# The last pass and the end of a fp32 decoder layer: last units bank by bank, layer norm by blocks of tokens, rows of x1 put in order in DRAM, and the mLSTM state products spread over the main products

## The chip, the cores and the metric

One NeuronCore of a Trainium2 chip. The metric is the device time of one execution in microseconds (us). The kernel is written instruction by instruction: a scheduler in Python fixes, at build time, the order of instructions on each engine (TensorE = PE, VectorE = DVE, ScalarE = ACT, GpSimd = POOL, and SyncE = SP, which only issues DMAs here). On the chip each engine runs its list in order and waits on semaphores.

## The reference

One layer on 320 tokens (256 of a prompt, 64 = 8 sequences × 8 of a sample batch), D = 2048, all float32. Cut to what matters:

```python
proj = x @ w_in                      # split: mLSTM q,k,v,i,f,o; HGRN2 q,f,i,g; two gates
h, C, n, m = _mlstm(q, k, v, ig, lf, C0, n0, m0)     # 4 heads, dk 256, dv 512, chunks of 64
o, S = _hgrn2(hq, log f, 1 - f, i, S0)               # 8 heads, dk 128, dv 256
merged = sigmoid(gate_a) * (branch_a @ w_branch_a) + sigmoid(gate_b) * (branch_b @ w_branch_b)
x1 = layernorm(alpha * x + merged @ w_out)
hid = square(relu(x1 @ w_up))                        # 2048 -> 8192
y = layernorm(alpha * x1 + hid @ w_down)             # 8192 -> 2048
# outputs: y, and the new states C, n, m, S of prompt and sample
```

For the prompt the new states are `C = k_scaled^T v` and `S = k_scaled^T i` over all 256 tokens: one product over the tokens for each head.

## The kernel before, in words

**Products.** A float32 product is done as three products of rounded halves: each operand is split into a high and a low part, and high×high, high×low and low×high are summed in a PSUM bank. The weights come from DRAM in tiles of 128 × 1024 (512 KB) into six raw buffers, all by SP's queue (`reload`). ACT writes the high half (`highs`, by the helper at L415), DVE the low half (`lows`, L681). The (high, low) pairs lie in a small pool, `wh`, `wl` and `bb` in the names below. `give` says where a pair's buffer goes once PE is done with it: back to the pool, or, near the end, to the pools for k and v (`kx`, `vx`).

**Main products.** `run_main` walks a list of units: first weight tiles of the projections ("w"), then the MLP with down projections in passes p = 0 to 7. The first seven passes have the kinds A, B and C (a scheme with seven products instead of eight, summed up later by `combine`). The last pass has the kinds D and E: 16 units in the order D g0 ×4, E g0 ×4, D g1 ×4, E g1 ×4, where g is a half of the output columns. Each such unit has one weight tile and 16 products of 512 columns into three PSUM banks: 4 for the samples' tokens (block 2), 6 for tokens 0 to 127 (block 0) and 6 for tokens 128 to 255 (block 1). Four units share three banks, so each bank is complete only in the fourth unit. `ev_last` then adds a bank to the sum of the earlier passes, adds the residual's part (put there by `residual`) and takes the statistics; `norm` (L2457 to L2467) applies the layer norm and stores y, once for the samples' block and once for both prompt blocks together, after the last statistics.

**x1 for the residual.** x1 is kept in DRAM (`xD`), written from a transposed layout, so that a token's row lies there in pieces of 32 floats (128 bytes). `residual` fetches the rows back with twelve DMAs of such pieces on SP's queue at the start of the last pass, and g2 and b2 with two more.

**States.** k and v of the four mLSTM heads and the operands of the eight HGRN2 heads also wait in DRAM (`kD`, `vD`, `sD`, `iD`). `m_C(h)` asks for k (L1370) and v (L1373) by POOL's queue when `kx` and `vx` have buffers, then waits until the main products are done (`main_end`), and does 12 products of 512 columns; `C_out` copies a bank by ACT and stores it by SP. `h_S(h)` does S of a head in four products of 256 columns, and it waits for C of all four heads.

**Order.** Each of these functions is a chain, a Python generator that yields an engine, a cost and an instruction, or a wait. The scheduler places ready chains by priority beside the main products, and the estimated times it works with fix the order only. They put no waiting time into the program. POOL's queue carries nothing but a few memsets and the loads of k and v.

Of the kernel before, what the change touches and what calls it, by code (L numbers as in the profile page):

```python
# [8 lines left out]
F32 = mybir.dt.float32  # L9
# [327 lines left out]
PE_C = 2000.0  # L337
PE_H = 1250.0


# [36 lines left out]
class Program:  # L377
# [312 lines left out]
    def run_main(self):  # L690
# [3 lines left out]
        for u, unit in enumerate(UNITS):  # L694
            if unit[0] != "w":
                self.down(u, *unit)
                continue
# [40 lines left out]
    def down(self, u, kind, p, g, i):  # L738
        s = self.s
        if (kind, g, i) == ("A", 0, 0) and p == 0:  # L740
            s.spawn(self.open_dn(), 0)
        if (kind, p, g, i) == ("A", PH - 2, 0, 0):
            for j in range(2):
                s.spawn(self.combine(j), 1)
        if (kind, g, i) == ("D", 0, 0):
            self.carve_end()
            now = s.t["pe"]
            self.vx.free.append((now, self.brest))
            self.kx.free += [(now, self.wxv[4].rearrange("p x s v -> p (x s v)")[:, 1024 * i:1024 * i + 1024]) for i in range(2)]
# [39 lines left out]
        s.pump(s.t["pe"])  # L789

    def take(self):
        s = self.s
        s.until(lambda: self.mbank.free)
        self.mbank.free.sort(key=lambda x: x[0])
        at, b = self.mbank.free.pop(0)
        s.t["pe"] = max(s.t["pe"], at)
        return b

    def give(self, u):

        now, hl = self.s.t["pe"], self.unit[u][0]
        n = [hl is w for w in self.wx].index(True) if any(hl is w for w in self.wx) else 0
        if n > 1 and u >= U_MLP - 6:
            if self.wide_done is None:
                self.wide_parts(self.wxv[n], now)
            else:
                self.wide_done.append(self.wxv[n])
        elif u >= len(UNITS) - 3 or n < 2 and any(hl is w for w in self.wx) and u > len(UNITS) - 16:
            if any(hl is w for w in self.wx):
                self.vx.free.append((now, self.wxv[n]))  # L810
            else:
                self.kx.free += [(now, x) for x in hl]
        elif self.hlp is not None:
            self.hlp.free.append((now, hl))
        else:
            self.hl_free.append((now, hl))
# [62 lines left out]
    def start(self):  # L879
# [22 lines left out]
        self.s_ev = {(x, c): Ev() for x in range(3) for c in range(4)}  # L902
        self.xD = self.dr.tile([32, 4, KT * TOK], F32, name="xD")
        self.used_ev = [Ev() for _ in range(KT)]
        first = d["first"]
# [461 lines left out]
    def m_C(self, h):  # L1367
        k = yield acq(self.kx)
        k = k.rearrange("p (x s k) -> p x s k", x=2, s=2)
        kt = yield ("pool", 1000, lambda: self.nc.gpsimd.dma_start(  # L1370
            k.rearrange("p x s k -> p (x s k)").rearrange("p (y k) -> p y k", k=128), self.kD[h].rearrange("y p k -> p y k")))
        w = yield acq(self.vx)
        vt = yield ("pool", 1000, lambda: self.nc.gpsimd.dma_start(w, self.vD[h]))  # L1373
        e = Ev()
        e.t = max(kt, vt) + 4000.0
        yield wait(e, self.main_end)
        for c in range(2):
            b = yield acq(self.mbank)
            for s in range(2):
                yield ("pe", 3 * pe_r(512), lambda: [self.mm(  # L1380
                    b, k.rearrange("p x s k -> p (x s k)")[:, 512 * x + 256 * c + 128 * s:512 * x + 256 * c + 128 * s + 128], w[:, y, s, :],
                    start=s == 0 and n == 0, stop=s == 1 and n == 2) for n, (x, y) in enumerate(((0, 0), (0, 1), (1, 0)))])
# [529 lines left out]
    def h_S(self, h):  # L1912
# [4 lines left out]
        e.t = t  # L1917
        yield wait(e, *[m["C"] for m in self.mh])
        b = yield acq(self.mbank)
# [324 lines left out]
    def spill_x1(self):  # L2244
# [11 lines left out]
        yield post(self.f3_ev)  # L2256

    def ev_up(self, T, p, b):
        v = self.nc.vector
# [118 lines left out]
    def residual(self):  # L2378

        v, d = self.nc.vector, self.d  # L2380
        T1, T2, TS = self.er
        x = self.xD.rearrange("r a (j b c) -> r (a j) b c", b=10, c=32)
# [20 lines left out]
        now = self.s.t["dve"]  # L2403
        self.sx.free += [(now, self.erest[:, 768 * i:768 * i + 768]) for i in range(6)]
        self.oS.free += [(now, self.erest[:, 4608 + 256 * i:4864 + 256 * i]) for i in range(2)]

# [22 lines left out]
    def ev_last(self, n, g, x, bank):  # L2429
# [7 lines left out]
        yield wait(self.w_ev[c][x])  # L2437
        rows = 128
        if x == 2:
            t = yield acq(self.ts)  # L2440
            rows = 64
            yield ("act", act(512), lambda: self.A(t[0:64], W[64:128]))
            yield ("dve", SUM, lambda: v.tensor_tensor(W[0:64], W[0:64], t[0:64], ALU.add))
            yield rel(self.ts, t)
        yield ("dve", SUM, lambda: v.bn_stats(self.st[:rows, x, c, :], W[:rows]))
# [4 lines left out]
    def norm(self, xs):  # L2450

        v = self.nc.vector
        yield wait(*[self.s_ev[x, c] for x in xs for c in range(4)])
        rows = 64 if xs == (2,) else 128
        n = len(xs)
        for x in xs:
            yield ("dve", 90, lambda: v.bn_aggr(self.mv[:rows, x, :], self.st[:rows, x].rearrange("p c n -> p (c n)")))  # L2457
        sm = yield acq(self.sm)
        yield from self.rsqrt(sm[:rows], self.mv[:rows, xs[0]:xs[0] + n, 1], n=n)
        G, B = self.gb2  # L2460
        for j, x in enumerate(xs):
            m, r = self.mv[:rows, x, 0:1], sm[:rows, 9 + n + j:10 + n + j]
            for c in range(4):
                W = self.last(c, x)[:rows]
                cc = slice(512 * c, 512 * c + 512)
                yield ("dve", SUM, lambda: v.scalar_tensor_tensor(W, W, m, G[:rows, cc], ALU.subtract, ALU.mult))
                yield ("dve", SUM, lambda: v.scalar_tensor_tensor(W, W, r, B[:rows, cc], ALU.mult, ALU.add))  # L2467
                yield ("sp", 620, lambda: self.dma(self.d["y"][128 * x:128 * x + rows, cc], W))

# [104 lines left out]
```

## Time and profile before

| | us |
|---|---|
| median of 3 runs | 2263.31 (2261.55 to 2263.45) |
| profiled execution: time | 2264.3 |
| profiled execution: span of instructions | 2262.5 |
| TensorE busy | 2247.8 (99%) |
| VectorE busy | 1687.1 (75%) |
| ScalarE busy | 1277.1 (56%) |
| GpSimd busy | 12.6 (1%) |
| mean granted TensorE clock | 0.997 |

The span runs from the first to the last instruction; the execution's time has 1.8 us more. TensorE's row is the one to watch: it is nearly always busy, so the kernel's time changes where TensorE waits or is slowed. The DMA engines moved 490.95 MB at a mean of 217 GB/s, nearly all by SP's queue (the row "q1"), 6.29 MB by POOL's (the row "q0").

### The profile page before, as it was taken

The numbers are of one execution on the slowest core, as the hardware profiler recorded it, in microseconds if no ns is written. First come the engines' busy times: TensorE is split into PE (matmuls) and PEld (weight loads), VectorE is DVE, ScalarE is ACT, GpSimd is POOL, SyncE is SP. The second block draws the span as 40 slices with busy tenths as digits, with TensorE's granted clock in tenths as the row PEclk, the third lists the DMA queues.
The fourth block names the chain that finished last, engine by engine and source line by source line (L and its number), as shares of the span: only waits on it lengthen the run. The fifth ranks groups of instructions, "written<-read, shape, count | busy, mean of one in ns | idle before, by whom it ended". The sixth has DMA issues, their size and how long they took to land.

```text
span 2262.5 us, 37822 instructions
## 1 busy us (share of the span) xinstructions
PE 2247.8 (99%) x14316; PEld 2135.7 (94%) x14316; DVE 1687.1 (75%) x2982; ACT 1277.1 (56%) x2339; POOL 12.6 (1%) x36
## 2 busy tenths in 40 slices
PE   9999999999999999999999999999999999999997
PEld 9999999999999999999999999999999999999986
DVE  5676777777777787655655769888888888888876
ACT  6666556678777766444434438564555455555442
POOL 0000000000000000000000000000000000000000
PEclk9999999999999999999999999999999999999998
DMA  7598888756666676555555645867667676666697
GB/s 285 168 266 256 270 275 247 240 179 189 192 190 201 189 218 179 173 173 173 173 172 189 199 142 167 279 235 229 235 223 239 225 243 223 238 227 242 218 268 248
DMA packets 265535, 490.95 MB, mean 217 GB/s; under 512 B 119300, under 2 KB 145540, under 8 KB 264072
## 3 DMA queue, kind: packets, MB, share of 16 engines
q1 hardware_dynamic: 260472, 482.05, 67.2%
q0 software_dynamic: 4736, 6.29, 1.1%
q8 instruction: 112, 1.84, 0.3%
q14 instruction: 71, 0.58, 0.1%
q10 hardware_dynamic: 144, 0.20, 0.0%
HBM read 434.93 MB, written 53.53 MB: 216 GB/s over the span
## 4 chain that ended last, share of the span: by engine, by line
PE 97%; ACT 1%; issue 1%; DMA 0%; DVE 0%; POOL 0%; POOLq 0%; ACTq 0%
PE bank L421 97%; ACT f L415 1%; DMA xp<-vD 0%; ACT wh L415 0%; ACT ra L415 0%; DVE wl L616 0%; POOL wl L1370 0%; POOL wh L1370 0%; POOL bb L1373 0%; ACT f3h L415 0%; ACT rh L415 0%; PE bank L1101 0%; DVE f L1766 0%; DVE f L1578 0%; DVE f3h L1886 0%
## 5 line engine op out<-in xcount | busy, mean ns | idle before, releaser
L421 PE MATMUL bank<-xh,wh 128*128 128x320 f32 (+1 forms) x2680 | 841.6, 315 | 0.0
L421 PE MATMUL bank<-xh,wl 128*128 128x320 f32 (+1 forms) x2680 | 829.1, 310 | 0.0
L421 PE MATMUL bank<-xl,wh 128*128 128x320 f32 (+1 forms) x2680 | 825.9, 309 | 0.0
L415 ACT ACTIVATE wh<-wr 128x1024 fp32r<-128x1024 f32 x430 | 452.0, 1056 | 336.2 <-PE bank L421 262.2
L616 DVE TENSOR_TENSOR wl<-wr,wh 128x1024 fp32r<-128x1024 f32 x329 | 402.6, 1224 | 299.2 <-ACT wh L415 297.8
L421 PEld LDWEIGHTS bank<-xh,wh 128*128 128x128 f32 x2680 | 504.6, 188 | 10.6 <-issue 7.3
L421 PEld LDWEIGHTS bank<-xl,wh 128*128 128x128 f32 x2680 | 505.1, 189 | 4.3
L421 PEld LDWEIGHTS bank<-xh,wl 128*128 128x128 f32 x2680 | 505.2, 189 | 0.3 <-DVE wl L616 0.2
L421 PE MATMUL bank<-xh,bb 128*128 128x320 f32 (+1 forms) x784 | 177.9, 309 | 0.0
L681 DVE TENSOR_TENSOR wl<-wr,wh 128x1024 fp32r<-128x1024 f32 x101 | 122.1, 1219 | 37.6 <-ACT wh L415 37.5
L421 PE MATMUL bank<-wh,xp 128*128 128x512 f32 x434 | 144.7, 390 | 0.0
L415 ACT ACTIVATE f<-f 32x256 f32<-32x256 f32 (+6 forms) x339 | 120.7, 357 | 37.0 <-DVE f L1578 20.2
L421 PEld LDWEIGHTS bank<-xh,bb 128*128 128x128 f32 x784 | 132.5, 188 | 1.1
L421 PE MATMUL bank<-ra,wh 128*128 128x320 f32 x468 | 128.1, 309 | 0.0
L421 PE MATMUL bank<-xl,bb 128*128 128x320 f32 (+1 forms) x392 | 120.9, 308 | 0.0
L421 PE MATMUL bank<-bb,wh 128*128 128x320 f32 (+1 forms) x524 | 116.3, 311 | 3.4 <-DMA bb<-vD 3.4
L415 ACT ACTIVATE bb<-r 128x1024 fp32r<-128x1024 f32 (+1 forms) x84 | 81.9, 983 | 62.6 <-DVE r L663 42.1
L421 PE MATMUL bank<-wl,xp 128*128 128x512 f32 x284 | 110.6, 389 | 0.0
L415 ACT ACTIVATE bb<-wr 128x512 fp32r<-128x512 f32 (+1 forms) x110 | 95.9, 884 | 20.4 <-PE bank L421 9.0
L681 DVE TENSOR_TENSOR bb<-r,bb 128x1024 fp32r<-128x1024 f32 x70 | 85.4, 1220 | 28.7 <-ACT bb L415 28.7
L421 PE MATMUL bank<-bb,xp 128*128 128x512 f32 x430 | 104.0, 389 | 0.0
L421 PEld LDWEIGHTS bank<-bb,xp 128*128 128x128 f32 x430 | 80.6, 188 | 16.6
(378 smaller groups left out, 3484.9 us busy)
## 6 DMA issues: line engine op xcount, KB each, us to landing
wr<-wt SPq DMA_DIRECT2D x432, 512.0 KB, 3.7
wr<-wd SPq DMA_DIRECT2D x108, 512.0 KB, 4.8
r<-wd SPq DMA_DIRECT2D x88, 512.0 KB, 4.7
f2m<-wd SPq DMA_DIRECT2D x44, 512.0 KB, 4.3
r<-wt SPq DMA_DIRECT2D x28, 512.0 KB, 3.6
rx<-C SPq DMA_DIRECT2D x36, 256.0 KB, 5.0
Cs<-rx SPq DMA_DIRECT2D x36, 256.0 KB, 4.8
f<-C SPq DMA_DIRECT2D x28, 256.0 KB, 4.5
```

The source lines that it names most:

```text
L415: return self.nc.scalar.activation(out, in_, func, **kw)
L421: self.nc.tensor.matmul(*a, **kw)
L616: self.V().tensor_tensor(lo, raw, hi.bitcast(F32), ALU.subtract)
L681: t = yield ("dve", LO, lambda: v.tensor_tensor(lo, x, hi.bitcast(F32), ALU.subtract))
```

## The change

Six edits that hang together:

1. `m_C` of all heads is spawned at the start of the last pass (D g0) instead of E g0, and heads 0 and 1 don't wait for the main products' end any more: their 24 products stand among the main ones. k and v use buffers of other tiles (v as two halves, k buffers given back after use).
2. `down_last`: the last group (E g1, four units) is run bank by bank, block 2, then 0, then 1, each over the four weight tiles, instead of tile by tile. `give` keeps two more (high, low) buffers in the pool to the end.
3. `norm` runs for one block of tokens as soon as that block's statistics are there. The samples' block is normed on 128 partitions, half of the columns on each 64, which takes two small copies of the statistics and a second copy of g2 and b2 (`gbs`, four DMAs). The stores of y are chains of their own (`store`).
4. `unmix`: ten DMAs on POOL's queue copy `xD` into a new DRAM tensor `xE` in which each token's row is whole, 2048 pieces of 128 bytes each.
5. `residual` fetches whole rows from `xE` with four DMAs.
6. `h_S` waits for the end of the main products only, not for C.

```diff
+C_LAND = (18000.0, 9000.0)
...
+                if u < len(UNITS) - PAIRS:
+                    self.down(u, *unit)
+                elif u == len(UNITS) - PAIRS:
+                    self.down_last()
...
+        if (kind, p, g, i) == ("A", 2, 0, 0):
+            s.spawn(self.unmix(), 3)
...
         if (kind, g, i) == ("D", 0, 0):
             self.carve_end()
             now = s.t["pe"]
-            self.vx.free.append((now, self.brest))
+            self.vx.free.append((now, [self.brest[:, x] for x in range(2)]))
...
             s.spawn(self.residual(), 1)
+            for j in range(MH):
+                s.spawn(self.m_C(j), 1)
         if (kind, g, i) == ("E", 0, 0):
-            for j in range(MH):
-                s.spawn(self.m_C(j), 3)
...
+    def down_last(self):
+        s = self.s
+        us = range(len(UNITS) - PAIRS, len(UNITS))
+        kind, p, g, _ = UNITS[us[0]]
+        passes = PASSES[kind]
+        self.banks = [self.take() for _ in range(3)]
+        for b in (2, 0, 1):
+            jobs = [(u, name, o) for u in us for x, name, o in passes if x == b]
+            for n, (u, name, o) in enumerate(jobs):
...
+                for m, (l, w) in enumerate(three):
+                    self.mm(self.banks[b], l, w, start=..., stop=...)
+                    s.t["pe"] += 227.0
+                s.pump(s.t["pe"])
+            s.spawn(self.ev_block(kind, p, g, b, self.banks[b]), 0)
...
-        elif u >= len(UNITS) - 3 or n < 2 and any(hl is w for w in self.wx) and u > len(UNITS) - 16:
-            if any(hl is w for w in self.wx):
-                self.vx.free.append((now, self.wxv[n]))
-            else:
-                self.kx.free += [(now, x) for x in hl]
+        elif u >= len(UNITS) - PAIRS - 1:
+            self.vx.free.append((now, [x.rearrange("p (s v) -> p s v", s=2) for x in hl]))
...
     def m_C(self, h):
...
-        vt = yield ("pool", 1000, lambda: self.nc.gpsimd.dma_start(w, self.vD[h]))
+        for x in range(2):
+            vt = yield ("pool", 1000, lambda: self.nc.gpsimd.dma_start(w[x], self.vD[h][:, x]))
         e = Ev()
-        e.t = max(kt, vt) + 4000.0
-        yield wait(e, self.main_end)
+        e.t = max(kt, vt) + C_LAND[h > 1]
+        yield wait(e, *[self.main_end] * (h > 1))
...
+        yield rel(self.kx, kb)
         yield rel(self.vx, w)
...
     def h_S(self, h):
-        yield wait(e, *[m["C"] for m in self.mh])
+        yield wait(e, self.main_end)
...
+    def unmix(self):
+        x = self.xD.rearrange("r a (j b c) -> r (a j) b c", b=10, c=32)
+        for b in range(10):
+            t = yield ("pool", 1000, lambda: self.nc.gpsimd.dma_start(
+                self.xE[32 * b:32 * b + 32].rearrange("r (n c) -> r n c", c=32), x[:, :, b, :]))
+            e = Ev()
+            e.t = t + 25000.0
+            yield wait(e)
...
     def residual(self):
-        for b in range(8):
-            to = self.er[b // 4][32 * (b % 4):32 * (b % 4) + 32].rearrange("p (n c) -> p n c", c=32)
-            yield ("sp", 620, lambda: self.dma(to, x[:, :, b, :]))
-        for b in range(4):
-            to = TS[32 * b:32 * b + 32].rearrange("p (n c) -> p n c", c=32)
-            t = yield ("sp", 620, lambda: self.dma(to, x[:, 32 * (b // 2):32 * (b // 2) + 32, 8 + b % 2, :]))
+        for i, to in enumerate((T1, T2)):
+            yield ("sp", 620, lambda: self.dma(to, self.xE[128 * i:128 * i + 128]))
+        for g in range(2):
+            t = yield ("sp", 620, lambda: self.dma(TS[64 * g:64 * g + 64], self.xE[256:320, 1024 * g:1024 * g + 1024]))
...
+        for x, name in zip(self.gbs, ("g2", "b2")):
+            for g in range(2):
+                yield ("sp", 620, lambda: self.dma(x[64 * g:64 * g + 64], d[name][:, 1024 * g:1024 * g + 1024].to_broadcast([64, 1024])))
...
-        if c == 3 and x != 0:
-            yield from self.norm((2,) if x == 2 else (0, 1))
+        if c == 3:
+            self.s.spawn(self.norm(x), 1 + (2, 0, 1).index(x))
...
+            for g in range(2):
+                to, of = slice(64 - 64 * g, 128 - 64 * g), slice(64 * g, 64 * g + 64)
+                yield ("act", act(12), lambda: self.A(self.st[to, x, 2 * g:2 * g + 2, :], self.st[of, x, 2 * g:2 * g + 2, :]))
...
+        G, B = self.gbs if x == 2 else self.gb2
...
+            self.s.spawn(self.store(x, c, W), 0, self.s.t["dve"])
```

Where the instructions stand. POOL's list from its last memset on, before; `kD_111` to `kD_114` are k of heads 0 to 3, `vD_115` to `vD_118` v:

```order
L1653 MEMSET f_79 128x320 x8
L1370 DMA bb<-kD_111 128x8x128
L1370 DMA bb<-kD_112 128x8x128
L1373 DMA xp<-vD_115 128x2048
L1373 DMA bb<-vD_116 128x2048
L1370 DMA wh<-kD_113 128x8x128
L1370 DMA wl<-kD_114 128x8x128
L1373 DMA bb<-vD_117 128x2048
L1373 DMA xp<-vD_118 128x2048
```

and after:

```order
L1684 MEMSET f_79 128x320 x8
L2293 DMA xE<-xD 2048x32 x10
L1399 DMA bb<-kD_111 128x8x128
L1399 DMA bb<-kD_112 128x8x128
L1403 DMA xp<-vD_115 128x1024 x2
L1403 DMA xp<-vD_116 128x1024
L1399 DMA bb<-kD_113 128x8x128
L1403 DMA xp<-vD_116 128x1024
L1403 DMA wh<-vD_117 128x1024
L1403 DMA wl<-vD_117 128x1024
L1399 DMA bb<-kD_114 128x8x128
L1403 DMA xp<-vD_118 128x1024 x2
```

The ten copies of `unmix` stand between the memsets and the loads of k. The first waits for the DMAs that wrote `xD`, the next seven for nothing, the ninth and tenth for the first and second; no instruction paces them.

TensorE's list at the end of the main products, before (the first row is the MLP's last product, the rows of 512 columns behind it are C, those of 256 are S):

```order
L421 MATMUL bank_88<-wl,bb 128x512
L421 MATMUL bank_84<-xp,bb 128x512 x3
L421 MATMUL bank_89<-bb 128x512 x3
L421 MATMUL bank_84<-xp,bb 128x512 x3
L421 MATMUL bank_87<-bb,wh 128x512 x3
```

and before, the end of C and the start of S:

```order
L421 MATMUL bank_91<-xp,wl 128x512 x6
L421 MATMUL bank_88<-xp,wl 128x512 x6
L421 MATMUL bank_84<-wr 128x256 x2
L421 MATMUL bank_89<-wr 128x256 x2
```

After, from the MLP's last product on (bank_84 and the first bank_88 rows of 512 columns are C of head 2, bank_91 begins head 3):

```order
L422 MATMUL bank_85<-wl,bb 128x512
L422 MATMUL bank_84<-wh,bb 128x512
L422 MATMUL bank_84<-wl,bb 128x512
L422 MATMUL bank_84<-wh,bb 128x512
L422 MATMUL bank_88<-wr 128x256 x2
L422 MATMUL bank_84<-wh,bb 128x512
L422 MATMUL bank_84<-wl,bb 128x512
L422 MATMUL bank_84<-wh,bb 128x512
L422 MATMUL bank_87<-xhe 128x256 x2
L422 MATMUL bank_88<-wh,bb 128x512
```

Products of S, which stood behind all of C, now stand between those of C2 and C3; C of heads 0 and 1 has gone up among the main products.

SP's list at the start of the last pass, before (`wd` are weights of the down projection):

```order
L424 DMA r_13433<-wd 128x1024 x2
L424 DMA xhe<-xD 32x64x32 x4
L424 DMA wr<-wd 128x1024
L424 DMA xhe<-xD 32x64x32 x4
L424 DMA wr<-wd 128x1024
L424 DMA xhe<-xD 32x32x32 x2
L424 DMA wr<-wd 128x1024
```

and after:

```order
L425 DMA r_13434<-wd 128x1024 x2
L425 DMA xhe<-xE 128x2048 x2
L425 DMA xhe<-xE 64x1024 x2
L425 DMA wr<-wd 128x1024
L425 DMA xle<-g 128x2048
L425 DMA xle<-b 128x2048
L425 DMA wr<-wd 128x1024 x2
```

Four loads of whole rows stand where the loads of pieces stood among the weights.

More of the change, by code (lines that the diff above doesn't have):

```diff
@@ L789, in down @@
         s.pump(s.t["pe"])
+    def down_last(self):
[7 more added lines that the diff above has]
+            for n, (u, name, o) in enumerate(jobs):
+                (hi, lo), at = self.halves_of(u)
+                X = self.X[p, UNITS[u][3]]
+                for part in PARTS[kind]:
+                    s.until(lambda: X["ev" + part].t is not None)
+                    at = max(at, X["ev" + part].t + LAT)
+                s.t["pe"] = max(s.t["pe"], at)
+                x, wh, wl = X[name], hi[:, o:o + 512], lo[:, o:o + 512]
+                three = [(x[0], wh), (x[1], wh), (x[0], wl)] if len(x) == 2 else [(x[0], wh), (x[0], wl)]
+                for m, (l, w) in enumerate(three):
+                    self.mm(self.banks[b], l, w, start=n == 0 and m == 0, stop=n == len(jobs) - 1 and m == len(three) - 1)
+                    s.t["pe"] += 227.0
+                s.pump(s.t["pe"])
+            s.spawn(self.ev_block(kind, p, g, b, self.banks[b]), 0)
+            s.pump(s.t["pe"])
     def take(self):
@@ L903, in start @@
         self.xD = self.dr.tile([32, 4, KT * TOK], F32, name="xD")
+        self.xE = self.dr.tile([TOK, D], F32, name="xE")
         self.used_ev = [Ev() for _ in range(KT)]
@@ L1367, in m_C @@
     def m_C(self, h):
[L1368 to L1369 removed]
+        kb = yield acq(self.kx)
+        k = kb.rearrange("p (x s k) -> p x s k", x=2, s=2)
         kt = yield ("pool", 1000, lambda: self.nc.gpsimd.dma_start(
@@ L2444, in ev_last, with norm @@
             yield rel(self.ts, t)
-        yield ("dve", SUM, lambda: v.bn_stats(self.st[:rows, x, c, :], W[:rows]))
+            W = V
+        yield ("dve", SUM, lambda: v.bn_stats(self.st[rows, x, c, :], W[rows]))
         yield post(self.s_ev[x, c])
-        if c == 3 and x != 0:
-            yield from self.norm((2,) if x == 2 else (0, 1))
-    def norm(self, xs):
+        if c == 3:
+            self.s.spawn(self.norm(x), 1 + (2, 0, 1).index(x))
+    def norm(self, x):
         v = self.nc.vector
[L2453 to L2457, printed above, removed]
-        sm = yield acq(self.sm)
[L2459 to L2468, printed above, removed]
@@ new lines, in norm @@
+        G, B = self.gbs if x == 2 else self.gb2
+        m, r = self.mv[:, x, 0:1], sm[:, 10:11]
+        for c in range(2 if x == 2 else 4):
+            W = self.last(c, x)
+            cc = slice(512 * c, 512 * c + 512)
+            yield ("dve", SUM, lambda: v.scalar_tensor_tensor(W, W, m, G[:, cc], ALU.subtract, ALU.mult))
+            yield ("dve", SUM, lambda: v.scalar_tensor_tensor(W, W, r, B[:, cc], ALU.mult, ALU.add))
+            self.s.spawn(self.store(x, c, W), 0, self.s.t["dve"])
@@ L2470, in run, with store @@
+    def store(self, x, c, W):
+        y = self.d["y"]
+        if x == 2:
+            for g in range(2):
+                cc = slice(1024 * g + 512 * c, 1024 * g + 512 * c + 512)
+                yield ("sp", 620, lambda: self.dma(y[2 * 128:2 * 128 + 64, cc], W[64 * g:64 * g + 64]))
+        else:
+            yield ("sp", 620, lambda: self.dma(y[128 * x:128 * x + 128, 512 * c:512 * c + 512], W))
     def run(self, pool):
```

24 lines of the change are left out of this document (15 added, 9 removed).

## The prediction

> **What bounds the kernel now.** I read the page first, then the end of the run by windows and by the timeline of TensorE, then the queues of GpSimd and SyncE, and last the DMA answers at the place where the new reordering will run.
>
> ```profile
> PE 2247.8 (99%) x14316; PEld 2135.7 (94%) x14316; DVE 1687.1 (75%) x2982; ACT 1277.1 (56%) x2339; POOL 12.6 (1%) x36
> PE 97%; ACT 1%; issue 1%; DMA 0%; DVE 0%; POOL 0%; POOLq 0%; ACTq 0%
> ```
>
> TensorE is busy for 99% of the span, and the chain that ended last is TensorE for 97%. A change that removes no product can win only where TensorE idles or runs at a lower granted clock, and it loses wherever it makes TensorE wait. So I look for the idle time, which stands at the end (start:end, length, busy time of PE, PEld, DVE, ACT, POOL, granted clock, DMA share, GB/s):
>
> ```profile
> 2168.50:2200.00 31.50, 31.50 (x141) 26.10 (x140) 17.92 (x26) 9.67 (x13) 0.54 (x1) 1.00 1.13 233
> 2200.00:2226.50 26.50, 26.50 (x118) 21.94 (x118) 22.89 (x33) 7.21 (x8) 2.33 (x3) 1.00 1.00 285
> 2229.00:2232.00 3.00, 0.00 (x0) 0.00 (x0) 2.90 (x10) 0.82 (x3) 0.00 (x0) 1.00 0.78 294
> 2232.00:2236.50 4.50, 4.37 (x12) 3.50 (x13) 1.14 (x2) 0.62 (x2) 0.00 (x0) 0.62 0.13 30
> 2240.00:2244.30 4.30, 0.12 (x1) 0.03 (x1) 4.20 (x7) 0.68 (x2) 0.00 (x0) 0.84 1.02 382
> 2244.30:2249.50 5.20, 5.20 (x12) 4.10 (x13) 5.06 (x9) 0.60 (x1) 0.00 (x0) 0.50 0.73 273
> 2249.50:2257.00 7.50, 7.22 (x33) 5.97 (x31) 2.13 (x3) 3.48 (x9) 0.00 (x0) 0.98 0.77 277
> 2257.00:2262.50 5.50, 0.00 (x0) 0.00 (x0) 0.00 (x0) 0.19 (x1) 0.00 (x0) 0.77 0.40 143
> ```
>
> Up to 2226.5 nothing is idle. Then come two holes of TensorE, each followed by a stretch at a granted clock of 0.62 and 0.50, and at the end 5.5 us without TensorE. The timeline of TensorE names them (start, length, engine, line, operation, count, idle time ahead and what ended it):
>
> ```profile
> 2226.33 0.39 PE L421 MATMUL bank<-wl,bb 128*128 128x512 f32 x1
> 2226.56 0.84 PE L421 MATMUL bank<-xp,bb 128*128 128x512 f32 x3
> 2227.24 0.84 PE L421 MATMUL bank<-bb 128*128 128x512 f32 x3
> 2232.13 1.16 PE L421 MATMUL bank<-bb,wh 128*128 128x512 f32 x3 [3.37 <-DMA bb<-vD]
> 2244.30 5.46 PE L421 MATMUL bank<-xp,wl 128*128 128x512 f32 x12 [4.18 <-DMA xp<-vD]
> 2249.56 2.84 PE L421 MATMUL bank<-wr 128*128 128x256 f32 x12
> 2252.24 1.03 PE L421 MATMUL bank<-f2m 128*128 128x256 f32 x4
> 2253.10 1.89 PE L421 MATMUL bank<-r 128*128 128x256 f32 x8
> 2254.83 1.89 PE L421 MATMUL bank<-xhe 128*128 128x256 f32 x8
> ```
>
> The first row is the last product of the MLP, so the main products end at 2226.56. From there to 2256.72 the tail does C of four heads and S of eight. Three products started 0.68 us after the three ahead of them, so one takes 0.2267 us; a head of C is 12 of them, 2.72 us. From 2252.24 to 2254.83 stand 12 products of S, 0.216 us each; all 32 are 6.91 us. Work in the tail is 4 × 2.72 + 6.91 = 17.8 us, and it takes 30.16 us: 12.4 us are holes and lowered clock. The holes are waits for v of heads 2 and 3, which GpSimd's queue asks for late:
>
> ```profile
> 2156.63 1.03 POOL L1370 DMA_DIRECT2D bb<-kD  x1 [1439.48 <-DMA f2m<-wd]
> 2183.50 0.54 POOL L1373 DMA_DIRECT2D bb<-vD  x1 [16.58 <-PE bank L421]
> 2221.29 0.57 POOL L1373 DMA_DIRECT2D bb<-vD  x1
> 2237.01 0.55 POOL L1373 DMA_DIRECT2D xp<-vD  x1 [15.14 <-PE bank L421]
> ```
>
> v of head 2 is asked for at 2221.29 and used at 2232.13, 10.8 us later; v of head 3 at 2237.01, when a buffer comes free, and used at 2244.30, 7.3 us later.
>
> **The change part by part.** *C of heads 0 and 1 among the main products, v buffers, S behind the main end.* No product is added or removed. 24 products of C move ahead of the last main product, which then ends at 2226.56 + 24 × 0.2267 = 2232.0. Behind it stand C2, C3 and S mixed: 24 × 0.2267 + 6.91 = 12.35 us, so without a hole TensorE ends at 2244.35, 12.37 us earlier than 2256.72. That needs the transfers to be there. A unit of the last pass is 16 products, 3.63 us. C0's products stand in the third unit of E g0, which begins ten units ahead of the main end, at 2190.3; its k was asked for at 2156.63 before, 33 us ahead. C1's stand in E g1 behind some 14 products, at about 2218; v1 is asked for when C0 leaves a buffer, at about 2196: 21 us. v2 goes into the buffer that the last D g1 unit leaves, at 2226.56 − 14.5 + 2.72 = 2214.8, and is used at 2232.0: 17 us. k3 and v3 go where C1 leaves its buffers. C1's 12 products end about 34 products after 2214.8, at 2222.5; with three issues at up to 1.03 us the last is out by 2224.5. C3's first product stands behind nine of C2 and two heads of S: 2232.0 + 2.04 + 1.73 = 2235.8, 11.3 us after that issue. The two rows above waited 10.8 and 7.3 us, so this holds, with 0.5 to 4 us to spare. GpSimd's waits delay nobody else: its queue holds only these.
>
> *The last group bank by bank.* The same products, 16 for the samples' block and 24 for each other block. The samples' bank closes 10.9 us ahead of the main end and block 0 5.4 us ahead. The fourth weight tile of the group is needed 8.2 us sooner in the group than unit by unit. Its buffer is one of two that now stay in the pool (five instead of three), so I cost it nothing: the cover is that two more tiles can be split ahead.
>
> *Norm by blocks.* VectorE works under TensorE, where it must end before 2244.35. Durations:
>
> ```profile
> 2228.82 0.68 DVE L2445 BATCH_NORM_STATS2 cst<-m 128x6 f32<-128x512 f32 x1
> L2467 DVE SCALAR_TENSOR_TENSOR m<-m,misc,xle 128x512 f32<-128x512 f32 (+1 forms) x8 | 6.0, 748 | 0.2
> ```
>
> After 2232.0 block 1 needs one add and one statistics (0.68 each), about 1.1 us of small ones, and eight of 0.75: 8.5 us. Block 0 began 5.4 us earlier with about the same 8.5 us, so 3.1 us of it may lie behind 2232.0: 2243.6 at the latest, under TensorE's end. The last y needs no more than S's last store. The samples' block now has four wide operations instead of eight narrow ones. The extra g2 and b2 loads (1 MB in four) go by SyncE behind the last weights.
>
> *The end.* What follows the last product:
>
> ```profile
> 2256.80 0.38 ACT L415 ACTIVATE m<-bank 128x256 f32<-128x256 f32 x1 [0.48 <-PE bank L421]
> 2257.64 0.88 SPq L424 DMA_DIRECT2D y<-m  x2
> ```
>
> Before, the last issue ended at 2258.52, 3.98 us ahead of the span's end. After: 2244.35 + 0.08 + 0.38 for ScalarE, about 0.4 for the issue, and the same 3.98: 2249.2. The span loses 13.3 us, if nothing else moves.
>
> *x1's rows put in order.* This adds ten transfers by GpSimd, DRAM to DRAM, of 2048 pieces of 128 bytes each. Twelve loads of the same pieces by SyncE become four of whole rows; TensorE had no idle time beside those loads (31.50 of 31.50), so dropping them gains nothing. The ten stand in GpSimd's queue ahead of the loads of k, where it sat idle for 1439 us, so only the writes of xD hold them; those end at about 1470, and eight of the ten go out without any wait. What do they meet there?
>
> ```profile
> 1470.00:1500.00 30.00, 30.00 (x168) 27.25 (x167) 25.16 (x36) 20.24 (x34) 0.00 (x0) 1.00 0.67 244
> 1476.83 0.33 SPq L424 DMA_DIRECT2D r<-wd  x1
> r<-wd SPq DMA_DIRECT2D x3, 512.0 KB, 4.9
> 1482.55 0.68 DVE L661 TENSOR_TENSOR f2m<-f2m,r 128x512 f32<-128x512 f32 x1
> 1481.41 1.22 DVE L681 TENSOR_TENSOR wl<-wr,wh 128x1024 fp32r<-128x1024 f32 x1
> 1483.14 0.30 PE L421 MATMUL bank<-xh,wh 128*128 128x320 f32 x1
> q1 hardware_dynamic: 4190, 0.53, 90.0%
> q1 hardware_dynamic: 1446, 0.18, 122.8%
> 2165.69 2.66 SPq L424 DMA_DIRECT2D r<-wd  x2
> q0 software_dynamic: 484, 0.75, 149.2%
> q1 hardware_dynamic: 3, 0.01, 1.3%
> q0 software_dynamic: 765, 0.38, 98.9%
> q1 hardware_dynamic: 487, 0.24, 51.4%
> ```
>
> Weights take 0.67 of the DMA engines there, and they are hardly ahead: a tile asked for at 1476.83 lands in 4.9 us, at 1481.7, and is used at 1482.55; a low half ends at 1482.6 and its unit begins at 1483.1. I allow 2 us of lead in all, an estimate from these. How long do 20,480 pieces take? SyncE's 128-byte pieces went 4190 in the 4 us from 2177, and 1446 in the first of them: 19.5 us or 14.2 us for all. I take 14.2, the row without pauses between issues, since eight of the ten will queue up. How much do the weights get meanwhile? From 2170 to 2172 GpSimd's queue poured k and v; a weight tile asked for by 2168.35 waited, and SyncE's queue moved 3 packets, 1% of the busy time. From 2223 to 2225 it got 51.4 of 150.3, 34%. I take 20%, between the two. Then the pouring lasts 14.2 / 0.8 = 17.8 us, the weights fall behind by (0.67 − 0.20) × 17.8 = 8.3 us, and with 2 us of lead TensorE waits 6.3 us. Ends: 0.33 × 21.5 − 2 = 5.1 us at the 34% share, 0.66 × 19.5 − 2 = 10.9 us at 1% and the slower pieces. Nothing regains this, as TensorE has no other slack up to 2226. The lower end of the unknown is 0, if the pieces come over 43 us or more (14.2 / 0.33), and its upper end twice the piece time, since both sides of a piece lie in DRAM: 0.66 × 39 − 2 = 23.7 us.
>
> How the engines share decides between these. The Trainium skill's page "DMA: Bandwidth & Descriptors" (Queues, rings and completion order) says that each engine takes turns between the queues, a whole packet of some 9 to 17 descriptors (64 at most) at a turn. By that rule a turn of weight pieces would be longer than a turn of 128-byte pieces, and the weights would lose nearly nothing: the first rival. The row with 3 packets against 484 speaks against it.
>
> **The sum.** Span: 2262.5 − 13.3 + 6.3 = 2255.5. The profiled execution took 2264.3, 1.8 us more than its span, and the median of the runs is 2263.31, 1.0 below it; so 2255.5 + 1.8 − 1.0 = 2256.3 us.
>
> **The rivals.**
>
> - *The reordering is hidden.* GpSimd hands out pieces slowly, or the queues share so that the weights keep their 0.67. For it: 1024 pieces of k took 1.03 us to issue, so ten times 2048 are some 21 us and more, with gaps; a weight piece is 32 times as long as a piece of 128 bytes. Against it: 21 us are not 43, and the 3 packets. Time: 2263.31 − 13.3 = 2250.0, between 2248 and 2252.5.
> - *The reordering starves the weights*: slower or no change. A piece from DRAM to DRAM costs twice the row, or the weights get 1% of the engines. Its place is 1470 to about 1510. It decides from 8.8 us of waiting on (within 0.2%) and from 17.8 us on (slower): the 13.3 us saved plus or minus 4.5, the 0.2% that a measurement of this kernel can tell from no change. Time: with 15 us, near 2265; up to 2274. For it: the 1% row. Against it: the pouring of k and v held the weights up for the 2 us of its row, and TensorE did not wait then (31.50 of 31.50).
> - *The tail gets a hole again.* k3 and v3 come later than 11.3 us after their issue, since the extra loads and S's loads share the engines (share 1.00 from 2200 on). Then TensorE waits 1 to 3 us before C3, and after 3.37 us of idling the clock was 0.62 for 4.5 us, so 12 more products could cost 2.7 us more. Or VectorE or the stores end after TensorE. Either costs 1 to 6 us beside the forecast's 6.3: 2257 to 2262.
>
> **How the numbers follow.** Forecast (wait of 2.5 to 8.8 us in the middle, tail closed): chance 0.42, 2252.5 to 2258.8, all faster. Hidden: 0.22, all faster. Starved: 0.20, of it 0.12 within 0.2% and 0.08 slower. Hole in the tail: 0.16, of it 0.10 faster (below 2258.8) and 0.06 same. Faster 0.74, same 0.18, slower 0.08. The range 2249 to 2263 leaves out the fastest part of hidden (about 0.05) and most of starved (about 0.13).
>
> **What would show each step.** In the profile after: the last main product near 2232 plus the wait in the middle; behind it no TensorE idle time above 0.5 us and a granted clock of 1.00; from the last product of S to the end about 4.8 us. For the reordering: ten GpSimd issues near 1470 to 1490, and TensorE idle time of 2 to 9 us in all between 1470 and 1520, ended by weight transfers or by the splits behind them, with SyncE's queue well under 0.67 of the engines. No idle time there makes hidden right and the forecast 6 us too slow. Over 9 us makes starved right. TensorE idle before the product of C3 shows the hole, and a late unit in the last group would show the five buffers too few.

## The result

The changed kernel takes 2250.36 us (median of 4 runs, 2249.25 to 2251.12) against 2262.82 us of the kernel before (4 runs): a ratio of 0.9945, 95% interval 0.9928 to 0.9962, or 12.5 us less. The time is in the range and on the side that was forecast; it is the time of the rival "hidden" (2250.0) and not of the likeliest case (2256.3). The profiled execution took 2249.25 us, with a span of 2247.4.

The page of the changed kernel, busy time by engine:

```profile
PE 2242.0 (100%) x14316; PEld 2132.0 (95%) x14316; DVE 1685.8 (75%) x2982; ACT 1277.9 (57%) x2343; POOL 24.9 (1%) x50
```

The span lost 15.1 us and TensorE's busy time 5.8 us with the same 14316 products: the holes are gone, and so are the products at a lowered clock. (The two profiles lie further apart than the medians: the execution before, 2264.3 us, was slower than its other runs, and this one is the fastest of its four.) The end by windows (the columns as in the prediction):

```profile
2155.00:2190.00 35.00, 35.00 (x181) 30.73 (x180) 26.05 (x34) 16.36 (x22) 2.90 (x4) 1.00 1.07 350
2212.00:2230.50 18.50, 18.50 (x84) 15.31 (x83) 13.51 (x29) 3.69 (x10) 3.04 (x5) 1.00 1.07 309
2230.50:2243.30 12.80, 12.80 (x58) 10.56 (x56) 12.12 (x22) 5.49 (x13) 0.00 (x0) 1.00 0.78 285
2243.30:2247.40 4.10, 0.03 (x1) 0.00 (x0) 0.00 (x0) 0.38 (x1) 0.00 (x0) 1.00 0.58 205
```

From 2155 on TensorE is busy in every microsecond up to 2243.3, at a granted clock of 1.00; VectorE works under it for 12.12 of the last 12.8 us. TensorE's timeline at the end, and the last row of VectorE:

```profile
2230.49 0.39 PE L422 MATMUL bank<-wl,bb 128*128 128x512 f32 x1
2230.72 0.39 PE L422 MATMUL bank<-wh,bb 128*128 128x512 f32 x1
2231.40 1.02 PE L422 MATMUL bank<-wr 128*128 128x256 f32 x4
2234.52 0.85 PE L422 MATMUL bank<-xp,bb 128*128 128x512 f32 x3
2242.31 1.03 PE L422 MATMUL bank<-r 128*128 128x256 f32 x4
2242.19 0.75 DVE L2513 SCALAR_TENSOR_TENSOR m<-m,misc,xle 128x512 f32<-128x512 f32 x1
```

The first row is the last main product, the second begins C2, the third S, the fourth C3. GpSimd's queue:

```profile
1469.03 9.32 POOL L2293 DMA_DIRECT2D xE<-xD  x9 [753.19 <-DMA xD<-f3m]
1478.58 1.02 POOL L2293 DMA_DIRECT2D xE<-xD  x1 [0.23 <-PE bank L422]
2213.72 0.53 POOL L1403 DMA_DIRECT2D wh<-vD  x1 [16.39 <-PE bank L422]
2221.96 0.90 POOL L1399 DMA_DIRECT2D bb<-kD  x1 [7.17 <-PE bank L422]
2222.84 1.09 POOL L1403 DMA_DIRECT2D xp<-vD  x2
```

All ten copies go out in 10.6 us from 1469 on. v of head 2 is asked for at 2213.7 and v of head 3 by 2223.9, before the main products end. At the place of the copies, the engines by windows (first row), what the two queues moved from 1471 to 1474 (two rows) and from 1474 to 1488 (two rows), and the copies' packets from 1470 to 1489; the last row is a VectorE operation that waits for a weight tile:

```profile
1470.00:1490.00 20.00, 20.00 (x107) 17.77 (x106) 15.70 (x22) 13.06 (x23) 9.38 (x10) 1.00 0.95 303
q0 software_dynamic: 119, 0.42, 82.3%
q1 hardware_dynamic: 18, 0.07, 8.1%
q1 hardware_dynamic: 693, 2.56, 53.3%
q0 software_dynamic: 664, 2.16, 47.8%
q0 software_dynamic: 800, 2.62, 49.3%
1483.25 0.69 DVE L662 TENSOR_TENSOR f2m<-f2m,r 128x512 f32<-128x512 f32 x1 [2.07 <-DMA r<-wd]
```

TensorE did not wait; VectorE waited 2.07 us for this tile and 1.27 us for one at 1491.82. The copies went in 800 packets for 2.62 MB, not 20,480.

### The profile page after: what moved, and what is told of

Its sections match the earlier page's. It is cut to its first block, busy times and chain, and to the rows that moved or that the text cites. A ratio compares the mean times of both kernels' runs of the same rounds, so it can differ in the third digit from the quotient of the medians.

```text
span 2247.4 us, 37834 instructions
## 1 busy us (share of the span) xinstructions
PE 2242.0 (100%) x14316; PEld 2132.0 (95%) x14316; DVE 1685.8 (75%) x2982; ACT 1277.9 (57%) x2343; POOL 24.9 (1%) x50
## 4 chain that ended last, share of the span: by engine, by line
PE 98%; ACT 1%; issue 0%; DVE 0%; POOL 0%; POOLq 0%
PE bank L422 98%; ACT f L416 1%; ACT wh L416 0%; ACT ra L416 0%; DVE wl L617 0%; ACT f3h L416 0%; ACT rh L416 0%; PE bank L1130 0%; DVE f L1797 0%; DVE f L1609 0%; DVE f3h L1917 0%; ACT m L416 0%; ACT misc L416 0%; POOL ones L915 0%; DVE misc L1344 0%
## 5 line engine op out<-in xcount | busy, mean ns | idle before, releaser
L422 PEld LDWEIGHTS bank<-xh,wh 128*128 128x128 f32 x2680 | 504.2, 188 | 10.6 <-issue 7.3
L422 PE MATMUL bank<-bb,wh 128*128 128x320 f32 x512 | 112.6, 309 | 0.0
L422 PE MATMUL bank<-bb,xp 128*128 128x512 f32 x450 | 109.2, 389 | 0.0
```

What stands on the lines that cost most here:

```text
L422: self.nc.tensor.matmul(*a, **kw)
```

## The experiments

All times are medians. The kernel before ran beside each experiment, at 2261.3 to 2262.2 us, against 2262.8 beside the changed kernel; the changed kernel itself was not run again. The differences to it below are plain differences to 2250.4. Taken by the ratios to the kernel before, they would be 0.7 to 2.0 us larger, so they are good to about 2 us.

**Without the reordering.** `unmix` isn't spawned, and `residual` has its twelve loads of pieces again.

```diff
-        if (kind, p, g, i) == ("A", 2, 0, 0):
-            s.spawn(self.unmix(), 3)
...
-        for i, to in enumerate((T1, T2)):
-            yield ("sp", 620, lambda: self.dma(to, self.xE[128 * i:128 * i + 128]))
+        for b in range(8):
+            to = self.er[b // 4][32 * (b % 4):32 * (b % 4) + 32].rearrange("p (n c) -> p n c", c=32)
+            yield ("sp", 620, lambda: self.dma(to, x[:, :, b, :]))
...
```

> The changed kernel without the reordering: the residual comes again in twelve loads of 128-byte pieces on SyncE's queue. Theory A (the gain is in the tail alone, the reordering neither cost nor brought TensorE anything): the same as the changed kernel, 2250.4 us within 1 us, TensorE without idle time between 2150 and its last product. Theory B (the early loads of k and v and the earlier need of the last weight tiles left no room for pieces, 21 us of blocked issue before): TensorE idles 1 to 5 us in the last two groups, 2251.5 to 2256. Theory C (the reordering did cost some hidden time near 1470): faster by up to 1 us.

Measured: 2259.89 us (11 runs), 0.9996 of the kernel before (0.9987 to 1.0005). Nearly the whole gain is gone: the reordering is worth 9.5 us here, more than any of the three theories had. Two windows of this run, and below them the same two of the changed kernel; then rows of this run:

```profile
2170.00:2200.00 30.00, 30.00 (x134) 24.86 (x133) 16.95 (x23) 10.22 (x14) 1.97 (x3) 1.00 1.14 193
2200.00:2240.00 40.00, 35.46 (x155) 28.52 (x153) 27.98 (x44) 8.17 (x13) 3.04 (x5) 1.00 1.27 332
2170.00:2200.00 30.00, 30.00 (x134) 24.86 (x133) 23.30 (x34) 9.06 (x11) 1.97 (x3) 1.00 0.97 335
2200.00:2240.00 40.00, 40.00 (x179) 33.27 (x178) 31.63 (x58) 12.31 (x24) 3.04 (x5) 1.00 1.01 281
```

```profile
2168.29 12.48 SPq L425 DMA_DIRECT2D xhe<-xD  x4
2216.71 1.06 ACT L416 ACTIVATE wh<-r 128x1024 fp32r<-128x1024 f32 x1 [5.22 <-DMA r<-wd]
2236.97 0.75 DVE L2514 SCALAR_TENSOR_TENSOR f2m<-f2m,misc,xhe 128x512 f32<-128x512 f32 x1 [4.98 <-DMA xhe<-b]
2241.53 0.50 PE L422 MATMUL bank<-wh,bb 128*128 128x512 f32 x1 [4.72 <-ACT m L416]
```

While the pieces come in, from 2170 to 2200, the engines are full (share 1.14) and move 193 GB/s instead of 335: in 30 us that is 4.3 MB less. The Trainium skill's page "DMA: Bandwidth & Descriptors" (Specifications) asks for 512 bytes and more in a transfer for line rate; 193 against 335 GB/s agrees in kind. The weights of the last tile, g2 and b2 and the operands of S all land later; VectorE waits for the second copy of b2, ScalarE behind it in order, and TensorE 4.72 us for a bank that ScalarE must copy. TensorE itself is still busy while the pieces come: the bill arrives 40 us later. Not all of the delay is transfer time. VectorE adds the late residual until 2220.9 instead of 2198.8, the second copies go into its buffer, and in this run's list they stand behind most of S's loads: SyncE asks for b2 from 2225.43 on, in the changed kernel from 2200.90. How much of the 9.5 us is the slower transfer and how much this order of the list was not separated.

**g2 and b2 by another queue.** The run above, with the second copies of g2 and b2 by ScalarE's DMA queue.

```diff
-                yield ("sp", 620, lambda: self.dma(x[64 * g:64 * g + 64], d[name][...]))
+                yield ("act", 100, lambda: self.nc.scalar.dma_start(x[64 * g:64 * g + 64], d[name][...]))
```

> The run without the reordering (residual in 128-byte pieces, 2259.9 us), with one thing more: the second copies of g2 and b2 for the samples' block come by ScalarE's DMA queue instead of standing behind S's loads on SyncE's. In that run VectorE waited 2.20 and 4.98 us for these copies, ScalarE then 12.31 us for VectorE, and TensorE 4.72 us for a bank that ScalarE had to copy. Theory L (this chain is what the pieces cost): the 4.7 us hole and its lowered clock go and the time falls to 2252.5 to 2256 us; the wait for the last weights (5.22 us of ScalarE, under 2 us of TensorE) stays. Theory M (the DMA engines are simply behind by the pieces' time, whatever stands where): another wait takes its place, 2258.5 to 2261.

Measured: 2259.51 us (10 runs), 0.9991 of before (0.9982 to 1.0001): theory M's time. Rows of this run:

```profile
2227.83 0.60 ACT L416 ACTIVATE m<-bank 128x512 f32<-128x512 f32 x1 [10.95 <-DMA xhe<-b]
2239.76 0.50 PE L422 MATMUL bank<-wh,bb 128*128 128x512 f32 x1 [4.96 <-ACT m L416]
```

ScalarE now stands for 10.95 us while it issues g2 (from 2216.26) and b2 (from 2221.53), and TensorE's hole is 4.96 us instead of 4.72. The edit put a new wait on ScalarE, and b2 was still asked for 20 us later than in the changed kernel, so it doesn't prove that any order of the queues would fail; it shows that taking this transfer out of SyncE's line is not enough.

**The reordering alone.** The kernel before with `unmix` and the residual from `xE`.

> The kernel before with the reordering alone: ten GpSimd copies into rows and the residual from these rows. Theory A (neither cost nor gain): the time of the kernel before within 1 us, no TensorE idle time near 1470 to 1490, the two holes of the tail as before. Theory C (a hidden cost): 1 us or more slower. Theory G (rows free the queues at the last pass, and k and v land sooner): 1 to 3 us faster.

Measured: 2258.27 us (11 runs), 0.9985 of before (0.9976 to 0.9994): 3.4 us faster, theory G. In its profile, v of head 2 took 7.3 us to land instead of 10.7 and the hole ahead of C2 is gone; the one ahead of C3 is still there:

```profile
bb<-vD POOLq DMA_DIRECT2D x1, 1024.0 KB, 7.3
2231.40 0.55 POOL L1376 DMA_DIRECT2D xp<-vD  x1 [10.05 <-PE bank L421]
xp<-vD POOLq DMA_DIRECT2D x1, 1024.0 KB, 7.1
2238.64 4.57 PE L421 MATMUL bank<-xp,wl 128*128 128x512 f32 x12 [4.13 <-DVE m L2477]
```

The last row puts the wait down to VectorE, but these products read k and v alone. v of head 3 was asked for at 2231.40, when C0 left its buffer, and landed 7.1 us later, at 2238.5, 0.1 us ahead of the first product: it is v again that comes late.

**C of heads 0 and 1 behind the main end.**

```diff
-        yield wait(e, *[self.main_end] * (h > 1))
+        yield wait(e, self.main_end)
```

> The changed kernel, but C of heads 0 and 1 waits for the end of the main products again. Theory A (the holes went because C0 and C1 gave their buffers back 14 us and more ahead, so that v of heads 2 and 3 could be asked for in time): main products end 5.4 us earlier, at 2225.3; v of head 2 is asked for at about 2229 and v of head 3 at about 2237, so C3 finds a hole of 4 to 6 us, with a lowered clock behind it: 5 to 9 us above the changed kernel, 2255.5 to 2259.5 us. Theory D (S as filler between C does it): S covers the transfers, 2250.4 to 2252.5.

Measured: 2263.64 us (10 runs), 1.001 of before (1.0001 to 1.0019), 13.3 us above the changed kernel: theory A in kind, but twice its price.

```profile
2232.78 1.09 POOL L1403 DMA_DIRECT2D xp<-vD  x2
2239.32 0.56 POOL L1403 DMA_DIRECT2D wh<-vD  x1
2241.29 0.47 PE L422 MATMUL bank<-xp,bb 128*128 128x512 f32 x1 [2.60 <-DMA xp<-vD]
2243.05 5.06 PE L422 MATMUL bank<-xp,bb 128*128 128x512 f32 x11 [1.29 <-DMA xp<-vD]
2252.23 0.77 PE L422 MATMUL bank<-wh,bb 128*128 128x512 f32 x1 [4.11 <-DMA wh<-vD]
```

The expectation had v of head 2 asked for at about 2229; it was 2232.8, since C0 shares TensorE with S. So both heads have holes, 8.0 us in these rows, and their products behind the holes run at a lowered clock (0.56 from 2241 to 2252, 0.50 from 2252 to 2259).

**S behind all of C.**

```diff
-        yield wait(e, self.main_end)
+        yield wait(e, *[m["C"] for m in self.mh])
```

> The changed kernel, but S of every head waits for C of all four heads again. Theory A: C3's first product comes at 2232.8 instead of 2234.5, and k and v of head 3 landed at about 2232 in the changed kernel: no hole or one under 1 us, 2250.4 to 2251.5 us. Theory D (S as filler does it): a hole of 2 to 5 us ahead of C3, with a lowered clock: 2253 to 2258.

Measured: 2250.77 us (5 runs), 0.9953 of before (0.994 to 0.9967): the same as the changed kernel within what these differences are good for. S as filler is worth nothing that shows once C0 and C1 are early; there is no hole for it to fill.

**Both undone.** C0 and C1 behind the main end and S behind C.

> The changed kernel with both undone: C of heads 0 and 1 behind the main products, and S behind all of C. The last group bank by bank, the norm by blocks and the reordering stay. Theory A (the tail's holes are the gain): v of head 2 asked for at about 2228 and of head 3 at about 2231, holes of 4 to 8 us in all and lowered clock behind them, S last: 8 to 12 us above the changed kernel, 2258.5 to 2262.5 us. If the earlier norm were what gains (Theory K): at most 3 us above, up to 2253.5.

Measured: 2266.58 us (10 runs), 1.0025 of before (1.0015 to 1.0034): 16.2 us above the changed kernel and slower than before. Without the early C, S as filler is worth 2.9 us (2266.58 against 2263.64).

```profile
2229.65 1.09 POOL L1403 DMA_DIRECT2D xp<-vD  x2
2237.33 0.76 PE L422 MATMUL bank<-xp,bb 128*128 128x512 f32 x1 [6.14 <-DMA xp<-vD]
2247.77 0.77 PE L422 MATMUL bank<-wh,bb 128*128 128x512 f32 x1 [3.77 <-DMA wh<-vD]
```

Theory A, again above its price. v of head 2 is asked for at 2229.7, against 2221.3 before: the buffers that used to come free for it stay with the weights in the change (read from the code, not tested by itself). The earlier norm alone gains nothing here (theory K falls).

**The last group tile by tile**, with the norm by blocks:

```diff
-                if u < len(UNITS) - PAIRS:
-                    self.down(u, *unit)
-                elif u == len(UNITS) - PAIRS:
-                    self.down_last()
+                self.down(u, *unit)
```

> The changed kernel with the last group weight tile by weight tile again (all three banks complete in the last tile); the norm stays by blocks. Theory E (bank by bank is needed, since VectorE would have all three blocks behind the main end: some 21 us of work from 2230.7 on against 12.5 us of TensorE): VectorE ends at about 2252 and the last y 3.5 us later, 6 to 9 us above the changed kernel, 2256.5 to 2259.5 us. Theory F (VectorE has room enough): 2250.4 to 2251.5.

**The old norm**, with the last group bank by bank: `ev_last` and `norm` of before, without the second copies of g2 and b2.

> The changed kernel with the old norm: the samples' block on 64 partitions, both prompt blocks together after the last statistics; the last group still bank by bank. Behind the main end VectorE then has one add, two statistics and 16 operations of 0.75 us, 14 to 15 us against TensorE's 12.5: it ends at about 2246, and the last y about 3.5 us later: 1 to 3 us above the changed kernel, 2251.5 to 2253.5 us. If VectorE's end doesn't matter: 2250.4 to 2251.

**Both of them**, so that the early C, S behind the main end and the reordering are left:

> The changed kernel with the old norm and the last group weight tile by weight tile: left of the change are the early C, S behind the main end and the reordering. TensorE should have no hole and end near 2243.5. VectorE ended at 2250.5 with the norm by blocks and tile by tile; the old norm's eight narrow operations in place of four wide ones add 3 us: it ends at 2253 to 2254, the time is 7 to 9 us above the changed kernel, 2257.5 to 2259.5 us. If the order of the norm doesn't matter once the tile order is undone: 2256 like the run with that alone.

Measured: 2255.98 (9 runs), 2252.78 (5 runs) and 2258.19 us (10 runs), that is 0.9976 (0.9967 to 0.9986), 0.9964 (0.9949 to 0.9978) and 0.9985 (0.9975 to 0.9994) of before, and 5.6, 2.4 and 7.8 us above the changed kernel. The three last rows of VectorE, in this order:

```profile
2249.78 0.75 DVE L2510 SCALAR_TENSOR_TENSOR m<-m,misc,xle 128x512 f32<-128x512 f32 x1
2246.04 0.75 DVE L2506 SCALAR_TENSOR_TENSOR m<-m,misc,xle 128x512 f32<-128x512 f32 x1
2251.99 0.75 DVE L2503 SCALAR_TENSOR_TENSOR m<-m,misc,xle 128x512 f32<-128x512 f32 x1
```

TensorE ends near 2243.9 without a hole in all three; the time follows VectorE's end. By the medians the parts add, 5.6 + 2.4 = 8.0 against 7.8; by the ratios it is 7.0 + 4.3 against 9.0, so they add within the 2 us only. Theory E holds, near the lower end of its price (6 to 9), and the prices for the other two (1 to 3 and 7 to 9) held.

**The reordering with short runs on both sides.** x1's rows padded in DRAM, 32 floats and 16 unused; `residual` reads them in such pieces too.

```diff
-        self.xE = self.dr.tile([TOK, D], F32, name="xE")
+        self.xE = self.dr.tile([TOK, 64, 48], F32, name="xE")
...
-                self.xE[32 * b:32 * b + 32].rearrange("r (n c) -> r n c", c=32), x[:, :, b, :]))
+                self.xE[32 * b:32 * b + 32, :, 0:32], x[:, :, b, :]))
...
```

> The changed kernel with rows of x1 padded in DRAM (32 floats, then 16 unused), so that the copies have 128-byte runs on both sides; the residual is then read in such pieces too. Tests the step of the prediction that failed. If the engines then move pieces of 128 bytes (Theory H: it was the joining of 32 pieces into one packet of 4096 bytes that spared the weights), 20,480 packets pour for 14 to 20 us or more, the weights get a small share, and TensorE idles 3 to 11 us between 1470 and 1510: 2253 to 2261 us. Theory I (the queues take turns and the weights have lead enough whatever the pieces): no idle time there, 2250 to 2251.5.

Measured: 2261.75 us (10 runs), 1.0001 of before (0.9992 to 1.001).

```profile
1470.00:1490.00 20.00, 16.40 (x82) 13.99 (x81) 11.67 (x16) 10.17 (x18) 10.02 (x10) 0.99 0.94 269
1489.85 0.64 PE L422 MATMUL bank<-xh,wl 128*128 128x320 f32 x1 [3.60 <-DVE wl L682]
q0 software_dynamic: 800, 2.62, 26.1%
```

The edit did not make what it was meant to make: the copies still went in 800 packets (last row, 1470 to 1510), so theory H isn't tested. Yet TensorE waited 3.60 us there and 0.94 us at 1501.56, and a copy took 12.0 us to land instead of 8.6. So theory I (no wait whatever the pieces) falls, and the cover over the reordering is thin. When the residual is first asked for, this run is 7.1 us behind the changed kernel (2174.49 against 2167.42); the other 4.8 us of its span come at the end, where the residual comes in pieces again, as in the first experiment. Why the copies into padded rows are slower stays open.

**The reordering three times**, twice into tensors that nobody reads:

```diff
-        for b in range(10):
+        for y in (self.xE, *self.xF):
+            for b in range(10):
...
-            e.t = t + 25000.0
+                e.t = t + 2000.0
...
```

The last edit moves the estimated time only, which lets the copies follow each other in GpSimd's list.

> The changed kernel with the reordering done three times (into two more tensors that nobody reads): the pouring doubled and more, about 55 us instead of 18. Theory J (the weights get 0.53 of the engines and need 0.67 to 0.7, and it was the lead of the weights that covered one round): they fall behind by some 0.15 us per us, 8 us after 55 us; less about 4 us of lead TensorE idles 2 to 6 us between 1490 and 1530: 2252 to 2257 us. Theory I (they are never short): 2250 to 2251.5.

Measured: 2258.68 us (10 runs), 0.9985 of before (0.9976 to 0.9994), 8.3 us above the changed kernel. Two windows, and the queues from 1470 to 1510:

```profile
1490.00:1510.00 20.00, 16.65 (x92) 15.45 (x90) 8.50 (x11) 6.67 (x12) 12.03 (x12) 0.91 1.03 345
1510.00:1530.00 20.00, 18.04 (x92) 15.25 (x93) 16.52 (x33) 14.21 (x26) 2.31 (x3) 1.00 0.97 350
q0 software_dynamic: 1855, 6.11, 49.1%
q1 hardware_dynamic: 1760, 6.42, 47.6%
```

TensorE idles 3.35 + 1.96 = 5.3 us, within theory J's 2 to 6, and the granted clock falls to 0.91 in the first window; the time lies 1.7 us above J's upper end. When the residual is asked for (2176.50) it is 9.1 us behind the changed kernel, nearly all of its loss. So the weights do fall behind while the copies pour; their lead covers one round and not three.

## Why the prediction was right, and where not

**The tail: right.** The holes came from late requests for v, and C of two heads among the main products took them away; in the run with them behind the main end the holes are back. (The reordering alone closes one of the two: v of head 2 lands sooner.) From the last main product to the last product of S, 12.35 us were forecast; the rows give 2230.72 to 2242.31 + 0.86 (four products) = 2243.17, 12.45 us. C3 was given 11.3 us after its last request; it had 2234.52 − 2223.93 = 10.6, and there was no hole. VectorE was to end by 2243.6 at the latest; it ended at 2242.94, 0.2 us under TensorE. From the last product to the span's end 4.8 us were forecast, 4.2 measured. The main products ended at 2230.72 instead of 2232.0. This lead of 1.28 us was there when the residual was asked for (2167.42 against 2168.70 before); about 1.0 us of it is the start (last section).

**The copies: the term of 6.3 us was 0.** SyncE's first load of the residual, 700 us behind the copies, begins at 2167.4 to 2168.3 in the eight profiles with one round of unpadded copies, and at 2168.2 to 2168.7 in the three without. Three sizes in the term were off. (1) "14.2 us for all", from SyncE's 128-byte pieces. The copies went in 800 packets, and these took 49.3% of 19 us of the engines, 9.4 us. (2) "The weights get 20%", a value between 1% and 34%. From 1474 to 1488 they got 53.3 against 47.8. The Trainium skill's page "DMA: Bandwidth & Descriptors" (Queues, rings and completion order) has the engines take turns between queues by packets; with packets of like size on both queues these rows, 693 packets against 664, agree with it, and the 3 packets against 484 that I set against it were met with k in many short pieces. The three microseconds ahead of these do not fit: 18 packets of weights against 119 of the copies, where the kernel before moved 84 of weights (1472.3 to 1475.3 there, 1.3 us later on its clock). Why stays open. (3) "2 us of lead". In the same stretches the weights took 0.42 and 0.645 of the engines before, less than the 0.67 that I had, so they fell behind by about (0.42 − 0.08) × 3 + (0.645 − 0.53) × 14 = 2.6 us. VectorE waited for them, 2.07 us at the most, and TensorE didn't: the lead is at least that. Three rounds used it up.

**"Dropping the piece loads gains nothing": wrong.** The step read TensorE's 31.50 of 31.50 beside those loads and stopped there. Alone, the reordering gains 3.4 us; together with the early C it carries 9.5 of the 12.5 us. The pieces fill the engines at 193 GB/s, and what they push back, by the engines and by the order of SyncE's list, is missed 20 to 60 us later.

**Bank by bank: right, but not priced by itself.** I had costed the earlier need of the fourth tile at nothing, and TensorE had no hole there; what the order gains by letting VectorE start earlier is 5.6 us, and the norm by blocks 2.4. My 13.3 us held these without naming their shares.

So the total came out near the "hidden" rival because its 13.3 us of tail were right, the 6.3 us set against them were not there, and the wrong "nothing" for the rows was hidden in a tail that I had taken to be free of holes anyway. That the range held the result was in part luck: the likeliest case rested on a wait that did not come, and it left out a gain that the closed tail needed.

## What to carry to other kernels

A busy bound engine beside a transfer does not show that the transfer is free: look at the GB/s in that window, and at who waits for a transfer in the 50 us behind it. When several edits close one tail, undo each one alone: here undoing any of three gives back much of the gain (13.3, 9.5 or 5.6 us of 12.5), more in sum than there was to gain, the norm by blocks 2.4, and S's place nothing that shows. Before pricing a rearranging copy by its pieces, find a row in which the same kind of copy (DRAM to DRAM, same queue) went, and if there is none, keep the whole packet as one of the ends.

## What the runs showed of the hardware

GpSimd's copies from DRAM to DRAM of 128-byte runs stand in the trace as 800 packets for 2.62 MB, whereas the same pieces that SyncE loaded into SBUF before went one by one (4190 packets for 0.53 MB). A GpSimd copy of 2048 runs took 1.03 us to issue, no more than a load of 1024 pieces of k before. And the first products differ between two profiled executions, the same group of three by 0.4 us and the row below by 1.0 us, without any edit there. Before, then after:

```profile
5.80 1.00 PE L421 MATMUL bank<-xl,wh 128*128 128x320 f32 x3
11.31 0.31 PE L421 MATMUL bank<-xh,wh 128*128 128x320 f32 x1
5.45 0.60 PE L422 MATMUL bank<-xl,wh 128*128 128x320 f32 x3
10.33 0.31 PE L422 MATMUL bank<-xh,wh 128*128 128x320 f32 x1
```

TensorE ran slower for longer at the start of the one execution; so a microsecond between two single profiles need not come from a change.
